# A decoder step on one core: where the values are stored from, who clears the padded attention tiles, and the pauses of the index list

## The chip, the cores and the metric

One core of a Trainium2 chip runs the whole program. The metric is device time in microseconds per execution; lower is better. Engines are named as in the profile: PE (TensorE, matmuls), DVE (VectorE), ACT (ScalarE), POOL (GpSimd), SP (SyncE, which here only issues DMAs).

## What is computed

Two layers over 256 prompt tokens and 8 x 4 sample tokens that share all weights (width 2048, float32). Layer 0 is sparse attention, layer 1 a Conformer convolution; each is followed by a ConvFFN and layer norms. The change lies in layer 0, and of it this matters:

```python
def one_seq(q_s, qi_s, wi_s, ki_s, k_new, v_new, pages):
    idx, valid = index_select(qi_s, wi_s, ki_s, pos_new, key_pos, k_sel)   # top 256 of 2052 keys, per token
    ...
    k_s = jnp.where(in_past, cache_k[phys, off], k_new[new_idx])
    v_s = jnp.where(in_past, cache_v[phys, off], v_new[new_idx])
    return attend_selected(q_s, k_s, v_s, valid)
```

For each of the 32 sample tokens an indexer scores 2052 keys and the best 256 are attended to; their keys and values lie in a paged cache and are gathered by row. The prompt tokens attend under a mask made from their own top 64. The new keys and values k, v are outputs as well.

## The kernel before

**Weights.** Every projection is a list of groups, each cut into slabs of 512 KB that SP loads into five buffers (`raw`). A float32 product is made of three passes over split operands: ACT makes the high part `wh` of a slab (L162), DVE or, for slabs marked `pool`, POOL makes the low part `wl` (L164), and PE multiplies (L231 to L233). `pump` issues loads five slabs ahead and splits up to three ahead, with three buffers for `wh` and `wl`.

**Order.** The order of the instructions on every engine is the order of the Python code; nothing is reordered later. While PE's matmuls are written, `tick` counts their nominal time as credit and runs generators in several lanes. A generator's `yield 2.5` means: go on after 2.5 us of credit. So the pauses set where the small work stands between the matmuls, on all engines, but each engine waits only for its data.

**The list of selected keys.** `sample_index` scores the keys, finds the 256th largest score by bisection (31 rounds on DVE with a small PE product each), and then, behind this threshold, makes the list: ranks among equals (L926), the selection (L929 to L933), a prefix sum (L939) with its count (L941), the sum of the counts on PE (L878, L948), nine compaction steps (L953 to L956), eight shift steps (L980, L981), a product on PE that puts the list together (L987) and the index tile `idxS` (L990). All this runs while PE multiplies the last slabs of q and of v.

**Gathers.** `kv_load` issues row gathers on POOL, two per token, each followed by a small memset as a pause, into a ring of 9 tokens: 4 buffers of `kvA` (two tokens until the projections end), 3 of `kvB`, and 2 in `kvx`, which takes over the memory of `xl`. A slot is refilled when its token's values have been used. `idxS` lets the first gather go.

**Values.** The projection's result is copied by ACT to `vT` (in the memory of `qi`), stored from there by SP, transposed by PE, and copied to `vt` and `vs`, which last through the attention. Then the pools of the indexer are closed, and the attention's tiles (`cp`) take over their memory.

**Attention.** A loop over the 32 tokens transposes the gathered keys (`keys`, L1207, copied out to `KT` by ACT at L1212 and DVE at L1210), makes scores of the token before (L1220 to L1228) with queries in the padded tile `qz` (L1313), and after four tokens a softmax and the values with padded weights in `PTz` (L1271). The padded tiles are cleared once (L1138), and later only their diagonals are written. Between these steps a filler does the prompt's attention: masked score products (L1156, L1157), maxima on DVE (L1158), exponentials on ACT (L1162), transposes (L1183, copied to `PT` by ACT), value products (L1179). The filler runs alone until `HEAD` us of its work are written, then the token loop starts.

Of the kernel before, what the change touches and what calls it, by code (L numbers as in the profile page):

```python
# [7 lines left out]
F32 = mybir.dt.float32  # L8
# [8 lines left out]
D = 2048  # L17
NT = 16
TP = 256
NS, TS = 8, 4  # L20
T = TP + NS * TS
NH, HD, NKV, GQ = 16, 128, 4, 4
NI, ID = 16, 64
# [3 lines left out]
FF = 5632  # L27
NF = FF // 128
CW = 31
# [8 lines left out]
NKVB = 3  # L38
# [8 lines left out]
KXD = (53.0, 4.8)  # L47
PRW = (6.0, 14.0, 9.0)
DOT = 0.35
HEAD = 3.0  # L50
DOTW = 5.0
PEM, NACT = 3, 4
BIS = (1.4, 0.3)
# [483 lines left out]
def trunk(ctx, tc, a, o, stages=9):  # L537
    k = K(ctx, tc, a, o)
    nc = k.nc
    base = k.base  # L540
# [6 lines left out]
    g_q = [k.add(Group([(win, QC + 512 * i, 512)], [128] * 4, NT, 2)) for i in range(4)]  # L547
    g_v = [k.add(Group([(win, VC + 256 * i, 256)], [128] * 2, NT, 4)) for i in range(2)]
    for g in g_q[1:]:
        for s_ in g.slabs[:8 if g is not g_q[3] else 4]:  # L550
            s_.pool = True
    def halving(w, nk):
        return [k.add(Group([(w, 512 * i, 512)], [128] * 4, nk, 2)) for i in range(3)] + \
# [40 lines left out]
    def hilo():  # L594
        xh = base.tile([128, NT, T + 2], F32R, name="xh")
        xl = base.tile([128, NT, T + 2], F32R, name="xl")
        return xh, xl

    xh, xl = hilo()
# [39 lines left out]
    def cc(n, p0=0, p1=128):  # L639
        o_, w_ = CO[n] if n in CO else CI[n]  # L640
        return (con if n in CO else coni)[p0:p1, o_:o_ + w_]
# [15 lines left out]
    def gather(out, src, idx):  # L657
        nc.gpsimd.indirect_dma_start(out=out, out_offset=None, in_=src,  # L658
                                     in_offset=bass.IndirectOffsetOnAxis(ap=idx, axis=0))
# [90 lines left out]
    kvt = {"pos": 0, "done": 0, "cap": 2}  # L750
    RING = 4 + NKVB + 2

    def kv_load(done):
        kvt["done"] += done
        while kvt["pos"] < min(kvt["done"] + kvt["cap"], NS * TS):
            t = kvt["pos"]
            i = t % RING - 4 - NKVB
            if i < 0:
                g = (kvA if i + NKVB < 0 else kvt["B"]).tile([128, 2, 1024], F32, name="kvt")
            else:  # L760
                g = kvt["B2"][:, i]
            kvt[t] = g
            for c in range(2):
                gather(g[:, c], a["kvc"], idxS[:, 32 * c + t:32 * c + t + 1])

                nc.gpsimd.memset(pause, 0)
            kvt["pos"] += 1
# [57 lines left out]
    def sample_index():  # L825
# [3 lines left out]
        p = pb()  # L829
# [13 lines left out]
        for pr in range(4):  # L843
# [3 lines left out]
            for i in range(4):  # L847
                p = pb()
# [8 lines left out]
        p = pb()  # L857
# [8 lines left out]
        p = pb()  # L866
# [7 lines left out]
        v = sp.tile([128, 1], I32, name="v", bufs=2)  # L874

        def total():
            p_ = pb()
            nc.tensor.matmul(p_[:, :1], cc("bones"), cnt, start=True, stop=True)  # L878
            return p_
# [3 lines left out]
        p = total()  # L883
# [9 lines left out]
        for bit in range(30, -1, -1):  # L893
# [8 lines left out]
            p = total()  # L902
# [5 lines left out]
        v = cand  # L908
# [8 lines left out]
        p = total()  # L917
# [6 lines left out]
        nc.vector.tensor_scalar(need, need, float(KSEL_S), None, op0=OP.add)  # L924
        rank = sp.tile([128, W1], I16, name="scr", bufs=2)
        nc.vector.tensor_tensor_scan(rank, eq, eq, 0.0, OP.add, OP.max)  # L926
        yield 2.5

        nc.vector.scalar_tensor_tensor(eq, rank, need[:, 0:1], eq, op0=OP.is_le, op1=OP.mult)  # L929
        nc.vector.tensor_tensor(gt, gt, eq, op=OP.add)  # L930
# [2 lines left out]
        nc.vector.tensor_tensor(mbS[96:128, KSEL_S:].rearrange("p (b t) -> p b t", t=TS),  # L933
                                new[96:128, None, :].to_broadcast([32, NS, TS]),
                                cc("blk", 96, 128).rearrange("p (b t) -> p b t", t=TS), op=OP.max)
        yield 2.0

        r = sp.tile([128, 512], I16, name="scr", bufs=2)
        nc.vector.tensor_tensor_scan(r, gt[:, :512], zer, -1.0, OP.add, OP.add)  # L939
# [3 lines left out]
        nc.vector.scalar_tensor_tensor(f, r, -32768.0, code, op0=OP.mult, op1=OP.add)  # L943
        x_ = sp.tile([128, 512], I32, name="x_", tag="w", bufs=3)
        nc.vector.tensor_tensor(x_, f, gt[:, :512], op=OP.mult)
        yield 1.5
        p = total()
        nc.tensor.matmul(p[:, 1:2], cc("lower"), cnt, start=True, stop=True)  # L948

        for b in range(9):  # L950
            s_ = 1 << b
            m = sp.tile([128, 512], I32, name="m_", tag="w", bufs=3)
            nc.vector.tensor_scalar(m, x_, 1 << (15 + b), None, op0=OP.bitwise_and)  # L953
            y = sp.tile([128, 512], I32, name="x_", tag="w", bufs=3)
            nc.vector.scalar_tensor_tensor(y, m, 0.0, x_, op0=OP.is_equal, op1=OP.mult)
            nc.vector.copy_predicated(y[:, :512 - s_], m[:, s_:], x_[:, s_:])  # L956
            x_ = y
            yield 2.6

        tot = sp.tile([128, 2], F32, name="tot")  # L960
        nc.vector.tensor_copy(tot, p[:, :2])
# [15 lines left out]
        for b in range(8):  # L977
            s_ = 1 << b
            y = sp.tile([128, KSEL_S], F32, name="lst", tag="w", bufs=3)
            nc.vector.tensor_scalar(y, lst, b0[:, b:b + 1], None, op0=OP.mult)  # L980
            nc.vector.scalar_tensor_tensor(y[:, s_:], lst[:, :KSEL_S - s_], b1[:, b:b + 1], y[:, s_:],  # L981
                                           op0=OP.mult, op1=OP.add)
            lst = y
            yield 1.2
        p = pb()
        for c in range(2):
            nc.tensor.matmul(p[:, 32 * c:32 * c + 32], lst[:, 128 * c:128 * c + 128], cc("bones")[:, :32],  # L987
                             start=True, stop=True)
        yield 0.7
        nc.vector.tensor_scalar(idxS, p[:, :64], 0.25, None, op0=OP.add)  # L990
        kv_load(0)

# [65 lines left out]
    vt = ap.tile([128, 2, 512], F32, name="vt")  # L1058
    vs = ap.tile([32, 512], F32, name="vs")
# [5 lines left out]
    for gi in range(2):  # L1065
# [4 lines left out]
        pl_.append(prompt_index(gi))  # L1070

    k.bg.append(sample_index())


# [9 lines left out]
    vT = bp.tile([128, 8, T], F32, name="qi")  # L1084

    def turn_v(gi):

        for tt in range(3):
            n = 128 if tt < 2 else 32
            p = pb()  # L1090
            for m in range(2):
                nc.tensor.transpose(p[:n, m * 128:m * 128 + 128], vT[:, 2 * gi + m, tt * 128:tt * 128 + n], ident)
            dst = vt[:, tt] if tt < 2 else vs
            nc.scalar.activation(dst[:, 256 * gi:256 * gi + 256], p[:n, :256], AF.Copy)
            yield 0.6

    for gi in range(2):
        ps = k.gemm(g_v[gi], xin, pg)
        for m in range(2):
            nc.scalar.activation(vT[:, 2 * gi + m], ps[m][:, :T], AF.Copy)  # L1100
        nc.sync.dma_start(o["v"].rearrange("(j p) t -> p j t", p=128)[:, 2 * gi:2 * gi + 2], vT[:, 2 * gi:2 * gi + 2])
        if gi:
            k.drain(k.ev, k.bg2, kxl, pl_, k.bg)
        pl_.append(turn_v(gi))
    k.drain(pl_)
    k.lanes.remove(kxl)
    k.lanes.remove(pl_)
    k.fine = False
# [7 lines left out]
    kvB = stC.enter_context(tc.tile_pool(name="kvB", bufs=NKVB))  # L1116
# [2 lines left out]
    def bank(n, bufs):  # L1119
        return pp.tile([128, 512], F32, name=n, bufs=bufs)  # L1120

    kvt["B"] = kvB
    kvt["cap"] = 4 + NKVB
    kv_load(0)


    ot = q
    kvt["B2"], kvt["cap"] = base.tile([128, 2, 2, 1024], F32, name="kvx", tag="xl"), RING
    kv_load(0)
    qz = [cp.tile([128, TS, NKV, 16], F32, name=f"qz{i}", bufs=1) for i in range(2)]  # L1130
    PTz = [cp.tile([128, 2, TS, NKV, 16], F32, name=f"PTz{i}", bufs=1) for i in range(2)]

# [2 lines left out]
        return bass.AP(tensor=t.tensor, offset=t.offset + off, ap=[list(t.ap[0]), [68, TS], [16, NKV], [1, GQ]])  # L1135

    for t in qz + PTz:
        nc.gpsimd.memset(t, 0.0)  # L1138

    def filler():  # L1140
        units = [(tt, h) for tt in range(2) for h in range(4)]
# [152 lines left out]

    while owed[0] < HEAD:
        r = next(fl)
# [548 lines left out]
    return a  # L1845


_OUT = {"y": (D, T), "k": (512, T), "v": (512, T), "kidx": (ID, T), "conv_p": (128, NT * (CW - 1)), "conv": (128, NT * NS * (CW - 1 + TS)), "ffn": (2, FF, 18)}


def build(a):
    import concourse.bacc as bacc
    nc = bacc.Bacc("TRN2", target_bir_lowering=False, num_devices=1)
    ins = {n: nc.dram_tensor(n, v.shape, mybir.dt.from_np(v.dtype), kind="ExternalInput").ap() for n, v in a.items()}
    outs = {n: nc.dram_tensor("out_" + n, s, F32, kind="ExternalOutput").ap() for n, s in _OUT.items()}
    with tile.TileContext(nc) as tc:
        with ExitStack() as ctx:
            trunk(ctx, tc, ins, outs)
    return nc


def _unlayout(r):
    c = np.ascontiguousarray
    t = lambda v: (v[:, :TP].T, v[:, TP:].T)
    yp, ys = t(r["y"])
    kp, ks = t(r["k"])
    vp, vs = t(r["v"])
    ip, is_ = t(r["kidx"])
    ff = r["ffn"]
    cp = r["conv_p"].reshape(128, NT, CW - 1).transpose(2, 1, 0)  # L1870
    cs = r["conv"].reshape(128, NT, NS, CW - 1 + TS)[..., TS:].transpose(2, 3, 1, 0)
    return (c(yp).reshape(1, TP, D), c(ys).reshape(NS, TS, D),
            c(kp).reshape(1, 1, TP, NKV, HD), c(vp).reshape(1, 1, TP, NKV, HD), c(ip).reshape(1, 1, TP, ID),
            c(cp).reshape(1, 1, CW - 1, D), c(ff[:, :, :2].transpose(0, 2, 1)).reshape(2, 1, 2, FF),
            c(ks).reshape(1, NS, TS, NKV, HD), c(vs).reshape(1, NS, TS, NKV, HD), c(is_).reshape(1, NS, TS, ID),
            c(cs).reshape(1, NS, CW - 1, D), c(ff[:, :, 2:].transpose(0, 2, 1)).reshape(2, NS, 2, FF))
# [8 lines left out]
```

## Time and profile before

| | us |
|---|---|
| median of 3 runs | 2647.25 (2644.3 to 2649.05) |
| the profiled execution, its own time | 2651.09 |
| its span, first to last instruction | 2649.3 |
| PE busy in the span | 2554.9 (96%) |
| DVE busy | 1623.9 (61%) |
| ACT busy | 1164.5 (44%) |
| POOL busy | 647.4 (24%) |

The times in the rows below are counted from the start of the span. A timeline row has the start, the length, the engine, the line and the operation with its output and inputs; in brackets stands how long the engine had stood before it, and what released it. The granted clock (PEclk) is 1.00 at 2.4 GHz and 0.50 at 1.2 GHz.

### The profile page before, as it was taken

The numbers are of one execution on the slowest core, as the hardware profiler recorded it, in microseconds if no ns is written. First come the engines' busy times: TensorE is split into PE (matmuls) and PEld (weight loads), VectorE is DVE, ScalarE is ACT, GpSimd is POOL, SyncE is SP. The second block draws the span as 40 slices with busy tenths as digits, with TensorE's granted clock in tenths as the row PEclk, the third lists the DMA queues.
The fourth block names the chain that finished last, engine by engine and source line by source line (L and its number), as shares of the span: only waits on it lengthen the run. The fifth ranks groups of instructions, "written<-read, shape, count | busy, mean of one in ns | idle before, by whom it ended". The sixth has DMA issues, their size and how long they took to land.

```text
span 2649.3 us, 49606 instructions
## 1 busy us (share of the span) xinstructions
PE 2554.9 (96%) x19608; PEld 2454.3 (93%) x19608; DVE 1623.9 (61%) x2536; ACT 1164.5 (44%) x1811; POOL 647.4 (24%) x921
## 2 busy tenths in 40 slices
PE   8999789999999999999998999899999999999997
PEld 8888556999999999999998889899999999999997
DVE  4577444777665445555558888779555444555554
ACT  4434334455444334344346444656444333444334
POOL 2033362342222101111036444344101000101123
PEclk9999899999999999999999999999999999999999
DMA  9834576456554455554645677455555445555643
GB/s 342 196 104 128 215 238 224 159 163 200 171 161 167 164 168 160 168 166 153 180 160 141 161 188 194 149 168 155 169 168 162 165 162 168 162 171 160 173 160 107
DMA packets 410553, 454.91 MB, mean 172 GB/s; under 512 B 34816, under 2 KB 338608, under 8 KB 409168
## 3 DMA queue, kind: packets, MB, share of 16 engines
q1 hardware_dynamic: 397920, 400.66, 49.4%
q0 software_dynamic: 12400, 51.09, 5.7%
q8 instruction: 153, 2.51, 0.4%
q14 instruction: 80, 0.66, 0.1%
HBM read 438.37 MB, written 13.30 MB: 170 GB/s over the span
## 4 chain that ended last, share of the span: by engine, by line
PE 89%; DVE 4%; POOL 2%; DMA 2%; ACT 1%; issue 1%; SPq 0%; ACTq 0%; DVEq 0%; POOLq 0%
PE pt L233 25%; PE pt L232 25%; PE pt L231 25%; PE pg L231 2%; PE pg L233 2%; PE pg L232 2%; PE pt L1671 1%; PE tr L1207 1%; DVE wl L164 1%; ACT wh L162 1%; PE m L1271 1%; POOL kvt L658 1%; DMA xt<-spread 1%; PE pg L849 1%; PE sc L1228 1%
## 5 line engine op out<-in xcount | busy, mean ns | idle before, releaser
L164 DVE TENSOR_TENSOR wl<-raw,wh 128x1024 fp32r<-128x1024 f32 (+2 forms) x705 | 879.3, 1250 | 781.0 <-ACT wh L162 768.3
L162 ACT ACTIVATE wh<-raw 128x1024 fp32r<-128x1024 f32 (+1 forms) x726 | 760.5, 1051 | 917.8 <-PE pt L232 682.1
L233 PE MATMUL pt<-xh,wl 128*128 128x288 f32 (+1 forms) x3520 | 1040.8, 296 | 4.1 <-DVE wl L164 4.1
L231 PE MATMUL pt<-xh,wh 128*128 128x288 f32 (+1 forms) x3520 | 1043.0, 296 | 0.8 <-ACT xh L1330 0.8
L232 PE MATMUL pt<-xl,wh 128*128 128x288 f32 (+1 forms) x3520 | 1043.1, 296 | 0.1
L233 PEld LDWEIGHTS pt<-xh,wl 128*128 128x128 f32 x3520 | 666.9, 189 | 5.1 <-DVE wl L164 5.1
L231 PEld LDWEIGHTS pt<-xh,wh 128*128 128x128 f32 x3520 | 664.1, 189 | 7.4 <-issue 5.8
L232 PEld LDWEIGHTS pt<-xl,wh 128*128 128x128 f32 x3520 | 664.6, 189 | 0.5 <-DVE xl L1331 0.3
L233 PE MATMUL pt<-hh,wl 128*128 128x288 f32 (+1 forms) x1664 | 495.4, 298 | 2.9 <-DVE wl L164 2.9
L231 PE MATMUL pt<-hh,wh 128*128 128x288 f32 (+1 forms) x1664 | 493.2, 296 | 1.2 <-ACT wh L162 1.2
L232 PE MATMUL pt<-hl,wh 128*128 128x288 f32 (+1 forms) x1664 | 493.2, 296 | 0.0
L1446 POOL COPY sto<-gpad 128x2 f32<-128x2 f32 x88 | 82.0, 932 | 962.1 <-ACT gpad L1439 962.0
L233 PEld LDWEIGHTS pt<-hh,wl 128*128 128x128 f32 x1664 | 312.7, 188 | 3.9 <-DVE wl L164 3.9
L231 PEld LDWEIGHTS pt<-hh,wh 128*128 128x128 f32 x1664 | 313.5, 188 | 2.4 <-ACT wh L162 2.1
L232 PEld LDWEIGHTS pt<-hl,wh 128*128 128x128 f32 x1664 | 313.9, 189 | 0.2
L231 PE MATMUL pg<-xh,wh 128*128 128x288 f32 (+1 forms) x528 | 167.1, 317 | 8.6 <-ACT wh L162 8.6
L233 PE MATMUL pg<-xh,wl 128*128 128x288 f32 (+1 forms) x528 | 158.0, 299 | 1.7 <-DVE wl L164 1.7
L232 PE MATMUL pg<-xl,wh 128*128 128x288 f32 (+1 forms) x528 | 158.0, 299 | 0.1
L1450 ACT ACTIVATE s<-y,pvec 128x304 f32<-128x304 f32 x88 | 48.5, 551 | 161.6 <-DVE y L1445 161.6
L231 PEld LDWEIGHTS pg<-xh,wh 128*128 128x128 f32 (+1 forms) x528 | 100.5, 190 | 17.9 <-ACT wh L162 8.8
L233 PEld LDWEIGHTS pg<-xh,wl 128*128 128x128 f32 (+1 forms) x528 | 100.4, 190 | 3.1 <-DVE wl L164 3.1
L232 PEld LDWEIGHTS pg<-xl,wh 128*128 128x128 f32 (+1 forms) x528 | 100.4, 190 | 2.9 <-issue 2.4
(377 smaller groups left out, 2323.2 us busy)
## 6 DMA issues: line engine op xcount, KB each, us to landing
raw<-w_ffn_gate SPq DMA_DIRECT2D x352, 256.0 KB, 2.9
raw<-w_ffn_up SPq DMA_DIRECT2D x352, 256.0 KB, 3.2
raw<-w_ffn_down SPq DMA_DIRECT2D x169, 512.0 KB, 3.5
raw<-w_attn_in SPq DMA_DIRECT2D x64, 512.0 KB, 5.7
raw<-w_pw SPq DMA_DIRECT2D x128, 256.0 KB, 4.5
raw<-w_attn_out SPq DMA_DIRECT2D x32, 512.0 KB, 5.3
raw<-w_pw SPq DMA_DIRECT2D x32, 512.0 KB, 3.6
xt<-spread SPq DMA_DIRECT2D x60, 136.0 KB, 2.9
```

The lines of the kernel that those rows point to most:

```text
L162: nc.scalar.activation(wh[:, :n], r[:, :n], AF.Copy)
L164: eng.tensor_tensor(wl[:, :n], r[:, :n], wh[:, :n].bitcast(F32), op=OP.subtract)
L231: nc.tensor.matmul(out, wh[:, c:c + w], xh, start=st, stop=False)
L232: nc.tensor.matmul(out, wh[:, c:c + w], xl, start=False, stop=False)
L233: nc.tensor.matmul(out, wl[:, c:c + w], xh, start=False, stop=sp)
L658: nc.gpsimd.indirect_dma_start(out=out, out_offset=None, in_=src, in_offset=bass.IndirectOffsetOnAxis(ap=idx, axis=0))
L849: nc.tensor.matmul(p[:, :512], qb[:, pr], kx[pr][:, 512 * i:512 * i + 512], start=True, stop=True)
L1207: nc.tensor.transpose(p[:, h * 128:(h + 1) * 128], g[:, h * 128:(h + 1) * 128], ident)
L1228: nc.tensor.matmul(p[32 * h:32 * h + 16, :KSEL_S], qz[b % 2][:, i, h], kt[:, h], start=False, stop=(i == TS - 1), skip_group_check=True)
L1271: nc.tensor.matmul(po[32 * h:32 * h + 16, :128], z[:, c, i, h], g[:, 512 + h * 128:640 + h * 128], start=False, stop=(i == TS - 1 and c == ...
L1446: nc.gpsimd.tensor_copy(sto[:, j, 0:2], gp[:, 256:258])
L1450: nc.scalar.activation(s[:, :304], y[:, :304], AF.Silu, bias=k.par(bc, j))
```

## The change

Six edits, all in the attention layer:

- the values are stored once, at the end of the projections, from `vt` and `vs`, in rows by token instead of by column (the host no longer transposes them); the store from `vT` is gone;
- `qz` and `PTz` are cleared by DVE instead of POOL, and in front of the gathers that follow the projections instead of behind them; the two calls of `kv_load` there become one;
- of the slabs of q's last group two instead of four are split by POOL, the other two by DVE;
- the first three pauses behind the threshold are 1.0 us longer each;
- the nine pauses of the compaction are 0.4 us shorter, the eight of the shifts 0.2 us, and the one in front of `idxS` is gone;
- `HEAD` is 2.0 instead of 3.0.

```diff
-HEAD = 3.0
+HEAD = 2.0
...
     for g in g_q[1:]:
-        for s_ in g.slabs[:8 if g is not g_q[3] else 4]:
+        for s_ in g.slabs[:8 if g is not g_q[3] else 2]:
             s_.pool = True
...
         nc.vector.tensor_tensor_scan(rank, eq, eq, 0.0, OP.add, OP.max)
-        yield 2.5
+        yield 3.5
...
-        yield 2.0
+        yield 3.0
 
         r = sp.tile([128, 512], I16, name="scr", bufs=2)
...
         nc.vector.tensor_tensor(x_, f, gt[:, :512], op=OP.mult)
-        yield 1.5
+        yield 2.5
         p = total()
...
             nc.vector.copy_predicated(y[:, :512 - s_], m[:, s_:], x_[:, s_:])
             x_ = y
-            yield 2.6
+            yield 2.2
...
             lst = y
-            yield 1.2
+            yield 1.0
         p = pb()
         for c in range(2):
             nc.tensor.matmul(p[:, 32 * c:32 * c + 32], lst[:, 128 * c:128 * c + 128], cc("bones")[:, :32],
                              start=True, stop=True)
-        yield 0.7
         nc.vector.tensor_scalar(idxS, p[:, :64], 0.25, None, op0=OP.add)
         kv_load(0)
...
             nc.scalar.activation(vT[:, 2 * gi + m], ps[m][:, :T], AF.Copy)
-        nc.sync.dma_start(o["v"].rearrange("(j p) t -> p j t", p=128)[:, 2 * gi:2 * gi + 2], vT[:, 2 * gi:2 * gi + 2])
         if gi:
             k.drain(k.ev, k.bg2, kxl, pl_, k.bg)
         pl_.append(turn_v(gi))
     k.drain(pl_)
+
+    nc.sync.dma_start(o["v"][:TP].rearrange("(a p) c -> p a c", p=128), vt)
+    nc.sync.dma_start(o["v"][TP:], vs)
...
+    for t in qz + PTz:
+        nc.vector.memset(t, 0.0)
+
+
     kvt["B"] = kvB
-    kvt["cap"] = 4 + NKVB
-    kv_load(0)
-
-
-    ot = q
     kvt["B2"], kvt["cap"] = base.tile([128, 2, 2, 1024], F32, name="kvx", tag="xl"), RING
     kv_load(0)
...
-    for t in qz + PTz:
-        nc.gpsimd.memset(t, 0.0)
...
-    vp, vs = t(r["v"])
+    vp, vs = r["v"][:TP], r["v"][TP:]
```

How it moves instructions shows at three places. The first is the start of the list on DVE, from the ranks to the count (`rsh` is the rope of q, `wl` a weight split). Before:

```order
L926 SCALAR_TENSOR_TENSOR scr<-eq 128x516
L722 STREAM_SHUFFLE rsh<-rsh 128x288
L723 TENSOR_TENSOR rsh<-rsh,con 128x288
L724 TENSOR_TENSOR rsh<-rsh,con 128x288
L726 TENSOR_TENSOR rsh<-rsh 128x288
L929 SCALAR_TENSOR_TENSOR eq<-scr,need,eq 128x516
L930 TENSOR_TENSOR gt<-gt,eq 128x516
L932 TENSOR_SCALAR new<-gt 32x4
L933 TENSOR_TENSOR mbS<-new,con 32x32
L939 SCALAR_TENSOR_TENSOR scr<-gt,zer 128x512
L941 TENSOR_SCALAR cnt<-scr 128x1
```

Now, the same piece:

```order
L926 SCALAR_TENSOR_TENSOR scr<-eq 128x516
L164 TENSOR_TENSOR wl<-raw,wh 128x1024
L722 STREAM_SHUFFLE rsh<-rsh 128x288
L723 TENSOR_TENSOR rsh<-rsh,con 128x288
L724 TENSOR_TENSOR rsh<-rsh,con 128x288
L726 TENSOR_TENSOR rsh<-rsh 128x288
L929 SCALAR_TENSOR_TENSOR eq<-scr,need,eq 128x516
L930 TENSOR_TENSOR gt<-gt,eq 128x516
L932 TENSOR_SCALAR new<-gt 32x4
L933 TENSOR_TENSOR mbS<-new,con 32x32
L164 TENSOR_TENSOR wl<-raw,wh 128x1024
L939 SCALAR_TENSOR_TENSOR scr<-gt,zer 128x512
```

The two splits that POOL made stand in DVE's order now, one ahead of the rope and one ahead of the scan; on PE the sum of the counts (L878) moves back by 24 matmuls, and L987 forward by 24.

The second place is DVE from the index to the filler's first maxima. Before:

```order
L990 TENSOR_SCALAR idxS<-pg 128x64
L1158 TENSOR_REDUCE mx<-tr 128x4
L1160 TENSOR_SCALAR mx<-mx 128x4
L1166 RECIPROCAL sm<-sm 128x4
L1168 TENSOR_SCALAR P<-P,sm 128x128 x4
```

Now:

```order
L989 TENSOR_SCALAR idxS<-pg 128x64
L164 TENSOR_TENSOR wl<-raw,wh 128x1024 x2
L1133 MEMSET qz_3176 128x256
L1133 MEMSET qz_3177 128x256
L1133 MEMSET PTz_3178 128x512
L1133 MEMSET PTz_3179 128x512
L1158 TENSOR_REDUCE mx<-tr 128x4
```

One split that stood ahead of the index stands behind it, and the four memsets, on POOL behind eighteen gathers before, stand on DVE ahead of the first maximum.

The third place is PE behind the projections, after the first eight score products of the filler. The difference:

```order
 L1157 MATMUL tr<-kT,x 128x128
-L1183 MATMUL tr<-ident,P 128x128 x4
-L1179 MATMUL q<-PT,vt 128x512
 L1207 MATMUL tr<-ident,kvt 128x128 x4
-L1156 LDWEIGHTS identN
-L1156 MATMUL tr<-pm,identN 128x128
-L1157 MATMUL tr<-kT,x 128x128
```

The first transposes of gathered keys (L1207) stand ahead of the transposes of the first softmax (L1183), where they stood behind its value product.

## Rows read from the trace of the kernel before

**Rows 1.** The page's chain that ended last, shares by engine.

```profile
PE 89%; DVE 4%; POOL 2%; DMA 2%; ACT 1%; issue 1%; SPq 0%; ACTq 0%; DVEq 0%; POOLq 0%
```

**Rows 2.** Windows of 5 us: length, PE, PEld, DVE, ACT, POOL busy (instructions), PEclk, DMA, GB/s.

```profile
235.00:240.00 5.00, 3.38 (x14) 3.41 (x15) 4.56 (x8) 0.00 (x0) 0.00 (x0) 0.50 0.41 120
...
295.00:300.00 5.00, 1.80 (x5) 1.14 (x6) 2.86 (x12) 2.36 (x12) 4.34 (x9) 0.61 1.04 416
...
305.00:310.00 5.00, 0.00 (x0) 0.00 (x0) 0.00 (x0) 0.00 (x0) 4.34 (x9) 0.97 1.02 419
...
315.00:320.00 5.00, 4.93 (x27) 2.29 (x27) 1.75 (x7) 2.62 (x9) 0.00 (x0) 0.50 0.40 163
```

**Rows 3.** Timeline, PE in the list: start, length, line, operation, [idle before <-releaser].

```profile
236.62 0.56 PE L878 MATMUL pg<-cnt,con 128*128 128x1 f32 x2 [5.17 <-DVE cnt L941]
...
282.94 0.70 PE L987 MATMUL pg<-con,lst 128*128 128x32 f32 x4
...
287.02 0.30 PE L233 MATMUL pg<-xh,wl 128*128 128x288 f32 x1
```

**Rows 4.** Timeline, DVE from the last split before the index.

```profile
285.12 1.22 DVE L164 TENSOR_TENSOR wl<-raw,wh 128x1024 fp32r<-128x1024 f32 x1 [1.94 <-ACT wh L162]
...
286.26 0.22 DVE L990 TENSOR_SCALAR idxS<-pg 128x64 int32<-128x64 f32 x1
...
292.80 0.69 DVE L1158 TENSOR_REDUCE mx<-tr 128x4 f32<-128x512 f32 x1 [6.32 <-DMA out_v<-qi]
...
312.99 1.20 DVE L1313 COPY qz<-qn 128x64 f32<-128x64 f32 x1 [12.94 <-POOL qz L1138]
```

**Rows 5.** Timeline, POOL: gathers and memsets.

```profile
286.76 1.07 POOL L658 DMA_INDIRECT kvt<-kvc,idxS  x1 [51.98 <-DVE idxS L990]
...
311.43 0.95 POOL L658 DMA_INDIRECT kvx<-kvc,idxS  x1 [0.17 <-issue]
...
312.62 0.58 POOL L1138 MEMSET qz<- 128x256 f32 x2
...
335.37 0.95 POOL L658 DMA_INDIRECT kvt<-kvc,idxS  x1 [21.23 <-PE m L1271]
```

**Rows 6.** Timeline, PE at the start of the attention.

```profile
289.13 0.22 PE L1156 MATMUL tr<-pm,identN 128*128 128x128 bf16 x1 [0.56 <-ACT vs L1094]
...
291.51 0.44 PE L1157 MATMUL tr<-kT,x 128*128 128x128 f32 x2
...
299.47 2.08 PE L1179 MATMUL q<-PT,vt 128*128 128x512 f32 x2 [2.25 <-ACT PT L1185]
...
315.07 1.11 PE L1183 MATMUL tr<-ident,P 128*128 128x128 f32 x4 [10.15 <-DVE KT L1210]
...
319.08 0.42 PE L1220 MATMUL sc<-mbS,selB 32*128 32x288 bf16 x1
...
343.60 1.09 PE L1207 MATMUL tr<-ident,kvt 128*128 128x128 f32 x8
```

**Rows 7.** Timeline, POOL's last weight split.

```profile
232.44 2.34 POOL L164 TENSOR_TENSOR wl<-raw,wh 128x1024 fp32r<-128x1024 f32 x1 [0.19 <-ACT wh L162]
```

**Rows 8.** Timeline, DVE at the start of the list.

```profile
227.51 0.48 DVE L722 STREAM_SHUFFLE rsh<-rsh 128x288 f32<-128x288 f32 x1
...
232.57 2.23 DVE L932 TENSOR_SCALAR new<-gt 32x4 bf16<-32x4 int16 x1
...
235.06 1.22 DVE L939 TENSOR_TENSOR_SCAN scr<-gt,zer 128x512 int16<-128x512 int16 x1
```

**Rows 9.** Timeline, ACT in the list and at token 0's keys.

```profile
228.29 1.08 ACT L162 ACTIVATE wh<-raw 128x1024 fp32r<-128x1024 f32 x1
...
229.44 1.84 ACT L729 ACTIVATE x<-rsh 32x288 f32<-32x288 f32 x4
...
302.44 0.60 ACT L1212 ACTIVATE KT<-tr 128x512 f32<-128x512 f32 x1 [0.26 <-issue]
```

**Rows 10.** Waits of DVE, 235 to 284 us: total, times, longest.

```profile
DVE wl L164 <- ACT wh L162: 3.8, 5, 1.9
```

More of the change, by code (lines that the diff above doesn't have):

```diff
@@ L1120, in bank @@
         return pp.tile([128, 512], F32, name=n, bufs=bufs)
-    kvt["B"] = kvB
-    kvt["cap"] = 4 + NKVB
-    kv_load(0)
     ot = q
-    kvt["B2"], kvt["cap"] = base.tile([128, 2, 2, 1024], F32, name="kvx", tag="xl"), RING
-    kv_load(0)
     qz = [cp.tile([128, TS, NKV, 16], F32, name=f"qz{i}", bufs=1) for i in range(2)]
@@ L1137, in trunk @@
     for t in qz + PTz:
-        nc.gpsimd.memset(t, 0.0)
+        nc.vector.memset(t, 0.0)
+    kvt["B"] = kvB
+    kvt["B2"], kvt["cap"] = base.tile([128, 2, 2, 1024], F32, name="kvx", tag="xl"), RING
+    kv_load(0)
     def filler():
@@ L1845, in _layout @@
     return a
-_OUT = {"y": (D, T), "k": (512, T), "v": (512, T), "kidx": (ID, T), "conv_p": (128, NT * (CW - 1)), "conv": (128, NT * NS * (CW - 1 + TS)), "ffn": (2, FF, 18)}
+_OUT = {"y": (D, T), "k": (512, T), "v": (T, 512), "kidx": (ID, T), "conv_p": (128, NT * (CW - 1)), "conv": (128, NT * NS * (CW - 1 + TS)), "ffn": (2, FF, 18)}
 def build(a):
```

## The prediction

> **What bounds the kernel now.** The page's chain of waits gives PE 89% of the span [rows 1], so an edit to the attention layer can only give time where PE stands. I looked for such places in the 5 us stretches, then followed each on the other engines.
>
> Two places show. In 235 to 240 us PE is busy 3.38 of 5.00 us at a granted clock of 0.50. Between 295 and 320 it does 1.80 of 5.00, then nothing in 305 to 310, and comes back at a clock of 0.50 [rows 2].
>
> At the first place PE waits 5.17 us for the count that the list's prefix sum makes on DVE [rows 3]. At the second, DVE stands 6.32 us at L1158 until the store out_v<-qi has landed, and 12.94 us at L1313 until POOL has cleared qz [rows 4]. POOL clears the tiles only after eighteen gathers, issued from 286.76 to 311.43 [rows 5]. Behind L1313 in DVE's order stand the copies that free PSUM, so PE waits 10.15 us at 315.07 [rows 6]. Transfers are no bound there: POOL has issued all it may and stands 21.23 us before the next gather [rows 5].
>
> **Part one, the list (222 to 287 us).** Two weight splits go from POOL to DVE, the first pauses get longer, the later ones shorter.
>
> The later of the two took 2.34 us on POOL [rows 7]; while it ran, DVE's L932, on 32x4 elements, took 2.23 us [rows 8], and L930 before it was long in the same way. Both get shorter, but this gives nothing, since the second moved split stands between them and the scan L939 and must wait for ACT. In order: ACT's wh runs from 228.29, 1.08, to 229.4 [rows 9]. The first split, 1.14 from start to start (L164 at 285.12 to the next at 286.26 [rows 4]), ends at 230.6. The rope, 1.93 from its first operation to ACT's L729 [rows 8, 9], brings 232.5; L729 x4, 1.84, 234.4; ACT's next wh 235.4; the second split 236.6. So L939 starts at 236.6 instead of 235.06 [rows 8], and the count, which let PE go 1.56 later at 236.62 [rows 3], is there at 238.1. The longer pauses put PE's sum of the counts 24 matmuls further back, 0.13 us each (27 between L987's end and 287.02 [rows 3]): PE comes there at 231.45 + 3.2 = 234.7 and stands 3.4 us instead of 5.17. That is 1.8 us, and up to 1.7 of clock (half of the 3.38 at 0.50).
>
> It does not last, since DVE sets the rest. From L939 to the end of PE's L987, which takes the finished list, passed 235.06 to 283.64, 48.6 us [rows 3, 8]; in 3.8 of them DVE waited for wh [rows 10]. With the pauses shortened one split fewer stands in between (1.1), and PE is ahead of DVE, so no wait for wh: 48.6 - 3.8 - 1.1 = 43.7. L987 ends at 280.3, 3.3 us earlier. But it stands 24 rows earlier in the value product, so PE waits there some 3 us, and 51 matmuls follow, 6.7 us: the last projection matmul ends at 287.1, against 287.3 now. **Term one: -0.2 us**; the 24 rows give back what the list gained. With no wait of PE at L987 it would be -3.5, with DVE's 3.8 of waits still there +3.6. I take the middle, because the list's rows leave DVE no gap.
>
> What the list does give is the index, no longer behind a split that waits for ACT: written at about 280.6 instead of 286.48, first gather at 280.9 instead of 286.76.
>
> **Part two, the attention's start (287 to 320 us).** The v store no longer reads qi, whose memory the attention's tiles take over, so DVE's first maximum waits only for PE: eight score products run from 289.13 to 291.95 [rows 6], four are through after 1.4 us, and with term one DVE starts at 288.9 + 1.4 = 290.3 instead of 292.80: 2.5 us.
>
> The four memsets stand on DVE just ahead. DVE has none in the trace. Below, they cost nothing beside that wait; above, four times the 0.69 of a 128x512 operation [rows 4] are 2.8. POOL's two qz took 0.58 [rows 5], the PTz have twice the elements: 1.7 in all, which I take, being the same tiles. They may start once PE has read qi for the last time, at 288.9 at the latest, and end by 290.6; so between nothing and 0.3 shows (1.4 at 2.8), and I take nothing. The Trainium skill (VectorE: DVE Perf Modes, section "Zero memsets can be issued as uint32 (trn2)") gives one cycle per element; 1536 elements at the skill's 0.96 GHz would be 1.6 us, an estimate from the page that no row here shows on DVE.
>
> From the first maximum to the end of the first value product passed 292.80 to 301.55, 8.75 us [rows 4, 6]; ACT now copies one KT tile, 0.60 [rows 9], ahead of PT, so it ends at 290.3 + 9.35 = 299.65. Then come eight key transposes (1.1, as at 343.60 [rows 6]) and four score products (1.4), and L1313 waits for nobody. Token 0's scores (L1220) begin at 302.15 instead of 319.08, 16.9 us earlier, term one among them. With HEAD at 2, one unit's transposes and value product are not done by then and follow later; their rows at the low clock are 1.11 and 2.08 [rows 6], half of that 1.6, with gaps 1.8. **Term two: -16.9 + 1.8 + 0.2 = -14.9 us.**
>
> The gathers keep up. The first of the second burst was issued at 335.37, and PE transposed it at 343.60 [rows 5, 6]: at most 8.2 us to land. So the first lands by 289.1, and PE wants it at 291.7. The eighteenth, 17 times 1.45 later, lands by 313.8; PE comes to token 9's keys 24.5 us behind token 0's scores [rows 6], to token 8's about 21, at 323. The v stores still carry 576 KB, now all of it beside the gathers; 288 KB more at 419 GB/s [rows 2] are 0.7 us, under that cover. Behind token 8 every refill waits for a token that PE has used, so the pattern moves as one. On SP the loads that no longer stand behind the store come earlier and nobody awaits them. All behind the layer is the same work.
>
> **Sum.** -0.2 - 14.9 = -15.1 us. The profiled execution took 2651.09 us (span 2649.3), 3.8 above the median of 2647.25; it would take 2636.0, and the median **2632**.
>
> **The rivals.**
>
> *More (0.14).* PE does not wait at L987, as DVE takes the list faster than its old rows say: 3.3 us more, and the clock of 0.61 in 295 to 300 stays at 1.00, some 2 us: 2627. Against it: the sum leaves DVE no gap.
>
> *Keys ahead of the first softmax (0.08).* PE takes its order as it stands, and token 0's key transposes now come before the first softmax's. If the first gather, with 288 KB of stores and weights beside it, lands 14 us after its issue instead of 8.2, that is at 294.9, PE stands 3.2 us; if the index is no earlier than before, 9 us: 2635 to 2641. Against it: the 8.2.
>
> *Nothing (0.05).* The wait only changes its name. The memsets wait for four of POOL's DMA queues. I read these as the index gathers of the start, since the first maximum waited for the same four and was released by the store. Were they the new gathers, DVE would stand until those land: gain 0 to 2, about 2646.
>
> *Slower (0.03): the clock.* PE's work after 289 comes in pieces with gaps. The granted clock was 0.61 in 295 to 300, where PE worked 1.80 of 5.00 us, and 0.50 in 315 to 320, after it had stood for ten, though it was then busy 4.93 of 5.00 [rows 2]. If it stays at the lower level, 1.2 GHz, from the first score product through token 8, the 21 us of work from token 0's scores take 42, and the 13 before some 3 more: -15.1 + 24 = +8.9, so 2656. It decides from the point where the gaps between tokens are as long as those around 295. Against it: once the keys are in, PE's next piece is always ready. The Trainium skill (TensorE: Matmul & The Clock Gate, Part 1) says "the default state is throttled, and activity releases the throttle"; by that rule a scattered start could hold the clock down, and the trace agrees as far as the 0.50 goes.
>
> **The numbers.** The forecast has 0.70. Its own range, from term one (-3.5 to +3.6), the memsets (1.4), the clock (2) and the runs' spread (2.4 either way), is 2626 to 2638. For 8 in 10 I take 2625 to 2641, which takes in the first two rivals but for a tail. A measurement can tell about 0.2%, 5.3 us: faster is under 2642, slower over 2652.5. Faster 0.70 + 0.14 + 0.07 = 0.91, same 0.06, slower 0.03.
>
> **What would show it.** Right: no wait of DVE on out_v or POOL between 285 and 320; PE's wait at L878 near 3.4 us, one at L987 near 3; first gather near 280.9; last projection matmul near 287; token 0's scores near 302; all behind token 8 some 15 us earlier. Wrong: a long wait of PE on a gather at the first key transposes, or of DVE at the memsets; the last projection matmul over 4 us off; or the 15 us given back behind token 8, where refills and not PE would set the pace.

## The result, and the profile after

| kernel | median of runs, us | range | profiled execution | its span |
|---|---|---|---|---|
| before | 2646.40 (6 runs) | 2643.76 to 2649.05 | 2651.09 | 2649.3 |
| after | 2632.98 (6 runs) | 2630.60 to 2634.12 | 2634.12 | 2632.3 |

The ratio is 0.9941, 95% interval 0.9931 to 0.9951: 13.4 us by the medians. The two profiled executions are 17.0 us apart, because that of before lies above all six of its runs; in which stage is shown below.

The changed kernel's 5 us stretches, in the columns of [rows 2]:

```profile
235.00:240.00 5.00, 1.62 (x10) 1.38 (x9) 3.58 (x5) 2.55 (x4) 0.00 (x0) 0.89 0.24 64
240.00:245.00 5.00, 5.00 (x21) 5.00 (x22) 4.18 (x6) 1.06 (x1) 0.00 (x0) 0.50 0.48 149
...
295.00:300.00 5.00, 1.94 (x9) 1.30 (x10) 3.30 (x13) 2.48 (x10) 4.50 (x7) 0.69 1.02 386
300.00:305.00 5.00, 5.00 (x22) 3.64 (x22) 1.40 (x3) 1.19 (x2) 4.34 (x9) 0.62 1.04 416
305.00:310.00 5.00, 4.09 (x47) 2.71 (x47) 3.05 (x8) 2.86 (x11) 3.71 (x6) 1.00 1.03 415
```

The stretch from 305 to 310, in which PE did nothing before, is 4.09 us busy now. What is left is in 295 to 305: two softmax steps in a row, and a granted clock of 0.69 and 0.62. DVE's timeline answers to [rows 4]:

```profile
281.86 0.22 DVE L989 TENSOR_SCALAR idxS<-pg 128x64 int32<-128x64 f32 x1 [0.50 <-PE pg L987]
...
290.15 0.55 DVE L1133 MEMSET qz<- 128x256 f32 x2 [2.42 <-PE pg L1091]
290.75 1.03 DVE L1133 MEMSET PTz<- 128x512 f32 x2
292.11 0.69 DVE L1158 TENSOR_REDUCE mx<-tr 128x4 f32<-128x512 f32 x1 [0.33 <-issue]
...
296.95 0.28 DVE L1313 COPY qz<-qn 128x64 f32<-128x64 f32 x1
```

Neither the wait for out_v nor the one for POOL is there. The clearings take 1.58 us and are over by 291.78, about when PE's first four score products are. PE's timeline, with POOL's behind it, answers to [rows 3, 5, 6]:

```profile
238.95 0.59 PE L878 MATMUL pg<-cnt,con 128*128 128x1 f32 x2 [3.38 <-DVE cnt L941]
...
281.12 0.70 PE L987 MATMUL pg<-con,lst 128*128 128x32 f32 x4 [1.19 <-DVE lst L980]
...
290.53 0.22 PE L1156 MATMUL tr<-pm,identN 128*128 128x128 bf16 x1 [0.56 <-ACT vs L1093]
...
293.19 0.60 PE L1207 MATMUL tr<-ident,kvt 128*128 128x128 f32 x4
...
295.88 0.79 PE L1183 MATMUL tr<-ident,P 128*128 128x128 f32 x4 [2.10 <-ACT P L1162]
...
298.85 1.11 PE L1207 MATMUL tr<-ident,kvt 128*128 128x128 f32 x4 [2.18 <-ACT P L1162]
...
299.82 2.08 PE L1179 MATMUL q<-PT,vt 128*128 128x512 f32 x2
...
305.00 0.29 PE L1220 MATMUL sc<-mbS,selB 32*128 32x288 bf16 x1
```

```profile
282.37 1.06 POOL L658 DMA_INDIRECT kvt<-kvc,idxS  x1 [54.96 <-DVE idxS L989]
...
307.73 0.94 POOL L658 DMA_INDIRECT kvx<-kvc,idxS  x1 [0.17 <-issue]
...
322.50 0.94 POOL L658 DMA_INDIRECT kvt<-kvc,idxS  x1 [13.45 <-PE m L1271]
```

Token 0's scores (L1220) start at 305.00, against 319.08 [rows 6]. PE finds its first keys ready at 293.19 (L1207, no wait in brackets); what it waits for now is ACT's exponentials, 2.10 and 2.18 us.

**Where the 17 us lie.** The two executions are already 0.93 us apart at L922, DVE's first operation behind the bisection, which the change leaves alone (224.98, 225.91). So every profile is counted from its own L922. The columns are starts, in us behind it: the first gather, the first score product (L1156), token 0's scores (L1220), the first value product of a request (L1271), the output projection (L231 on pt), and the end of the span. The "row stretch" is the time from L1271 to the output projection.

| profile | gather | score pr. | token 0 | L1271 | projection | end | row stretch |
|---|---|---|---|---|---|---|---|
| before | 61.8 | 64.2 | 94.1 | 109.5 | 214.2 | 2424.3 | 104.7 |
| after | 56.5 | 64.6 | 79.1 | 95.7 | 193.0 | 2406.4 | 97.3 |
| e13, before again | 61.9 | 64.2 | 94.1 | 109.6 | 204.4 | 2417.5 | 94.9 |
| e10, after again | 54.9 | 63.1 | 77.5 | 94.1 | 192.1 | 2404.9 | 98.0 |

The second profile of before agrees with the first to 0.1 us up to L1271, and is then 9.9 us shorter in the row stretch. So the apparent gain of 7.4 us there (104.7 to 97.3) does not belong to the change. After and e10 differ as well: by 1.6 us at token 0's scores, which goes back to the list and the clock in it (see "Why the prediction was right").

### The profile page after: what moved, and what is told of

It is laid out like the page before. It is cut to its first block, busy times and chain, and to the rows that moved or that the text cites. A ratio compares the mean times of both kernels' runs of the same rounds, so it can differ in the third digit from the quotient of the medians.

```text
span 2632.3 us, 49607 instructions
## 1 busy us (share of the span) xinstructions
PE 2553.5 (97%) x19608; PEld 2456.2 (93%) x19608; DVE 1624.8 (62%) x2542; ACT 1163.3 (44%) x1811; POOL 640.4 (24%) x915
## 4 chain that ended last, share of the span: by engine, by line
PE 87%; DVE 4%; DMA 3%; POOL 3%; ACT 2%; issue 1%; SPq 0%; ACTq 0%; DVEq 0%; POOLq 0%
PE pt L233 25%; PE pt L232 25%; PE pt L231 25%; PE pg L231 2%; PE pg L233 2%; PE pg L232 2%; DVE wl L164 1%; DMA kvt<-kvc,idxS 1%; PE pt L1671 1%; PE tr L1207 1%; ACT wh L162 1%; PE pg L849 1%; POOL x L489 1%; PE pg L1009 0%; PE m L1271 0%
## 5 line engine op out<-in xcount | busy, mean ns | idle before, releaser
L164 DVE TENSOR_TENSOR wl<-raw,wh 128x1024 fp32r<-128x1024 f32 (+1 forms) x707 | 882.0, 1251 | 783.0 <-ACT wh L162 770.9
L231 PE MATMUL pt<-xh,wh 128*128 128x288 f32 (+1 forms) x3520 | 1042.6, 296 | 0.8 <-ACT xh L1330 0.8
L231 PEld LDWEIGHTS pt<-xh,wh 128*128 128x128 f32 x3520 | 663.5, 189 | 7.8 <-issue 5.4
L231 PE MATMUL pt<-hh,wh 128*128 128x288 f32 (+1 forms) x1664 | 493.2, 296 | 1.2 <-ACT wh L162 1.2
L231 PEld LDWEIGHTS pt<-hh,wh 128*128 128x128 f32 x1664 | 313.6, 188 | 2.4 <-ACT wh L162 2.1
L231 PE MATMUL pg<-xh,wh 128*128 128x288 f32 (+1 forms) x528 | 168.3, 319 | 7.7 <-ACT wh L162 7.7
L231 PEld LDWEIGHTS pg<-xh,wh 128*128 128x128 f32 (+1 forms) x528 | 101.6, 192 | 16.9 <-issue 8.4
```

The source lines that it names most:

```text
L164: eng.tensor_tensor(wl[:, :n], r[:, :n], wh[:, :n].bitcast(F32), op=OP.subtract)
L231: nc.tensor.matmul(out, wh[:, c:c + w], xh, start=st, stop=False)
```

## The experiments

They ran in three batches, on three chips, on which the kernel before took 2656.5 us (e1 to e4), 2658.0 (e5, e6, e7, e9) and 2647.4 (e10 to e13); the ratios are against the kernel before on the same chip. The last three columns come from one profiled execution each, counted from L922 as above.

| run | what is different | median, us | ratio (95%) | token 0 | projection | row stretch |
|---|---|---|---|---|---|---|
| e1 | before, DVE clears | 2650.44 | 0.9978 (0.9969 to 0.9987) | 87.6 | 208.6 | 105.8 |
| e2 | before, store from vt, vs | 2655.77 | 0.9996 (0.9987 to 1.0005) | 94.2 | 214.5 | 104.8 |
| e3 | before, both | 2648.37 | 0.9972 (0.9961 to 0.9983) | 83.5 | 206.5 | 105.4 |
| e4 | before, list alone | 2651.27 | 0.9977 (0.9968 to 0.9986) | 90.6 | 213.6 | 107.3 |
| e5 | after, HEAD 3 | 2641.05 | 0.9943 (0.9929 to 0.9957) | 82.8 | 200.4 | 102.7 |
| e6 | after, POOL clears | 2640.52 | 0.9937 (0.9923 to 0.9950) | 77.2 | 203.0 | 106.3 |
| e7 | after, count later | 2642.17 | 0.9947 (0.9933 to 0.9961) | 79.0 | 204.0 | 107.3 |
| e9 | before, HEAD 2 | 2653.90 | 0.9991 (0.9982 to 1.0000) | 80.7 | 212.9 | 104.7 |
| e10 | after | 2633.25 | 0.9944 (0.9930 to 0.9958) | 77.5 | 192.1 | 98.0 |
| e11 | after, no pause | 2629.89 | 0.9931 (0.9919 to 0.9943) | 79.3 | 190.3 | 94.7 |
| e12 | after, old list | 2633.56 | 0.9945 (0.9933 to 0.9957) | 80.1 | 193.3 | 96.7 |
| e13 | before | 2648.01 | 1.0004 (0.9995 to 1.0012) | 94.1 | 204.4 | 94.9 |

**e1, VectorE clears.**

```diff
-        nc.gpsimd.memset(t, 0.0)
+        nc.vector.memset(t, 0.0)
```

> The kernel before, with one word changed: VectorE instead of GpSimd clears qz and PTz; store, list and HEAD as before. Theory A (the clearing behind the eighteen gathers is the bound, the store a smaller one ahead of it): DVE's wait for POOL at L1313 (12.94 us) is gone, the wait for out_v near 6.3 us stays and moves to the first clearing, the clearing itself (1.6 us) now shows: -12.9 + 1.6 = -11.3, so about 2635 against 2646. Theory B (clearing only hides a later wait, on the gathers or on PE's own order): under 3 us, 2643 to 2646.

6 us, half of what theory A expected. DVE's timeline in e1:

```profile
295.84 0.55 DVE L1138 MEMSET qz<- 128x256 f32 x2 [6.41 <-PE tr L1157]
296.44 1.02 DVE L1138 MEMSET PTz<- 128x512 f32 x2
297.38 0.63 DVE L1158 TENSOR_REDUCE mx<-tr 128x4 f32<-128x512 f32 x1
...
304.65 0.60 DVE L1313 COPY qz<-qn 128x64 f32<-128x64 f32 x1
```

POOL's wait is gone, as expected, and the store's wait has moved ahead of the clearing. The bracket names PE, but SP's timeline speaks for the store, in before and then in e1:

```profile
287.79 0.38 SPq L1101 DMA_DIRECT2D out_v<-qi  x1
```

```profile
290.75 0.38 SPq L1101 DMA_DIRECT2D out_v<-qi  x1
```

In before it was issued 5.0 us ahead of the maximum that it held (292.80), in e1 5.1 us ahead of the clearing (295.84). The size is not as expected: the 12.94 us were DVE's. PE, which sets the end, was still busy until about 305 in before and stood 10.15 [rows 6]. Take away the first maximum's delay of 2.3 us (70.1 against 67.8 behind L922) and some 8 are left; token 0's scores came 6.6 us earlier than in e2 beside it.

**e2, the store alone.**

```diff
-        nc.sync.dma_start(o["v"].rearrange("(j p) t -> p j t", p=128)[:, 2 * gi:2 * gi + 2], vT[:, 2 * gi:2 * gi + 2])
...
+    nc.sync.dma_start(o["v"][:TP].rearrange("(a p) c -> p a c", p=128), vt)
+    nc.sync.dma_start(o["v"][TP:], vs)
```

> The kernel before, with the value store from vt and vs alone; POOL still clears. Theory A: DVE's wait for out_v at L1158 (6.32 us) is gone and the first maximum comes near 290, but DVE then stands that much longer at L1313 for POOL, which still clears near 312.6: 0, within 1 us of 2646. Theory B (the store is what holds the start): -6, so 2640.

As theory A said: DVE's first maximum no longer waits for the store, and DVE's wait for POOL grows:

```profile
312.20 1.20 DVE L1315 COPY qz<-qn 128x64 f32<-128x64 f32 x1 [13.48 <-POOL qz L1140]
```

By itself the store gives 0.7 us, and the interval reaches past 1.

**e3, store and clearing:** the lines of e1 and of e2 together.

> The kernel before with both: store from vt and vs, VectorE clears; pauses, weight splits and HEAD as before. Theory A (the two waits add once both are gone, and list, splits and HEAD are worth next to nothing): -13 to -15, 2631 to 2633, the same as the whole change. Theory C (the part of the gain that shows only behind token 8, some 7 us in the profiles, comes from HEAD = 2, the order of prompt work and tokens): PE's small gaps behind token 8 stay, -8 to -10, 2636 to 2638.

The time, -8.1 us, is in the range of theory C; e5 and e9 test that theory directly.

**e4, the list alone:** in the kernel before, the pauses and the splits of the change.

```diff
-        for s_ in g.slabs[:8 if g is not g_q[3] else 4]:
+        for s_ in g.slabs[:8 if g is not g_q[3] else 2]:
...
-        yield 2.5
+        yield 3.5
...
-            yield 2.6
+            yield 2.2
```

> The kernel before, with the other pauses and the two weight splits on VectorE alone; store, clearing and HEAD as before. Theory A: PE waits 3.4 us instead of 5.2 at L878 and some 1.2 us at L987, the first gather is issued about 5 us earlier, POOL clears 5 us earlier (near 307.7 instead of 312.6), so DVE's wait at L1313 falls from 12.9 to about 8: -4 to -5, near 2641.5, by way of POOL and not of the list. Theory D (the list's own time counts): PE's last projection matmul 1 us later than in the kernel before and nothing else: 2646 to 2648.

-5.2 us, near what theory A said (-4 to -5), and by way of POOL. Timelines of POOL and of DVE in e4:

```profile
311.12 0.57 POOL L1137 MEMSET qz<- 128x256 f32 x2
```

```profile
311.48 1.20 DVE L1312 COPY qz<-qn 128x64 f32<-128x64 f32 x1 [7.73 <-POOL qz L1137]
```

DVE waits 7.73 us instead of 12.94. The earlier index lets POOL through its gathers earlier: it clears 84.2 us behind L922 instead of 87.6, 3.4 earlier (theory A said 5). The rest of the shorter wait is DVE's own: its first maximum came 1.6 us later. Token 0's scores come 3.5 us earlier (90.6 against 94.1); where the other 1.7 us of the time lie, this profile does not show. In the changed kernel nobody waits for POOL there, so this gain cannot be had a second time.

**e5 and e9, HEAD.** e5 is the changed kernel with the first line of this, e9 the kernel before with the second.

```diff
-HEAD = 2.0
+HEAD = 3.0
...
-HEAD = 3.0
+HEAD = 2.0
```

> The changed kernel with HEAD back at 3. Theory C (the gain behind token 8 comes from HEAD = 2; in the four runs with HEAD = 3 the stretch from the first value product of a request to the layer's output projection takes 104.7 to 107.3 us, in the changed kernel 97.3): that stretch goes back to about 105, and token 0's scores come 2 to 4 us later: 6 to 11 us slower than the changed kernel, so 2% is never in question but the ratio to the kernel before is 0.9965 to 0.9985 instead of 0.994. Theory A (store, clearing and list make the gain): within 1.5 us of the changed kernel.

> The kernel before with HEAD = 2 alone. Theory C: DVE still stands at L1313 until POOL has cleared (near 312.6), token 0's scores hardly move, and the stretch from the first value product of a request to the output projection falls from 105 to about 97 us: 5 to 8 us faster than the kernel before. Theory A: within 1.5 us of it.

Theory C falls: the changed kernel keeps its ratio with HEAD = 3 (0.9943; 2641.05 us, beside 2640.52 and 2642.17 in e6 and e7 with HEAD = 2), and HEAD = 2 alone gives 0.9 in a thousand, at the edge of the interval, with a row stretch of 104.7. In e9 token 0's L1220 runs early, at 80.7, but the scores behind it then wait for the keys, whose copy stands behind DVE's wait for POOL:

```profile
315.12 1.06 PE L1228 MATMUL sc<-KT,qz 128*16 128x256 f32 x8 [9.82 <-DVE KT L1210]
```

So the first value product (L1271) comes at 108.3, against 109.5. The profiles of e5 and e6, which also differ in who clears, show what HEAD does in the changed kernel: with HEAD = 2 token 0's scores are 5.6 us earlier (77.2 against 82.8), and by the output projection all of it has been given back (203.0 against 200.4). The edit of HEAD gives the whole nothing that these runs can tell.

**e6, POOL clears at the new place.**

```diff
-        nc.vector.memset(t, 0.0)
+        nc.gpsimd.memset(t, 0.0)
```

> The changed kernel with GpSimd clearing again, at the new place ahead of the second load of rows (so behind eight gathers and not eighteen). If the place is what counts: POOL clears near 294 to 296, DVE waits for nothing at L1313, DVE's 1.6 us of clearing ahead of the first maximum are gone, ten gathers go out 1.7 us later: within 1.5 us of the changed kernel. If the engine is what counts: DVE waits for POOL again, 3 us slower or more.

The place counts, not the engine: 0.9937 (0.9923 to 0.9950) against 0.9944 (0.9930 to 0.9958) for the changed kernel itself (e10, on another chip). POOL's timeline in e6:

```profile
288.14 0.56 POOL L1133 MEMSET qz<- 128x256 f32 x2 [1.21 <-ACT vt L1093]
288.64 1.00 POOL L1133 MEMSET PTz<- 128x512 f32 x2
...
289.80 0.94 POOL L658 DMA_INDIRECT kvt<-kvc,idxS  x1 [0.15 <-issue]
```

It clears behind four gathers (the expectation said eight) and in the same time as DVE, 1.56 us.

**e7, the count later.**

```diff
-        p = total()
-        nc.tensor.matmul(p[:, 1:2], cc("lower"), cnt, start=True, stop=True)
         for b in range(9):
...
-            yield 2.2
+            yield 2.4
+        p = total()
+        nc.tensor.matmul(p[:, 1:2], cc("lower"), cnt, start=True, stop=True)
         tot = sp.tile([128, 2], F32, name="tot")
```

> The changed kernel, with PE's sum of the counts (L878) issued behind the nine steps of the list that do not need it, and those steps' pause at 2.4 instead of 2.2. Theory E (PE's 3.4 us at L878 and the low clock behind it are lost for nothing): no wait at L878, some 2 to 4 us at L987, the first score product 2 to 4 us earlier, and the same at the end. Rival F (the attention's start then waits for the first gather, which lands 4 us or more behind its issue, or for the exponentials of ACT): the first score product earlier, token 0's scores not, 0 to 1 us in all.

Neither theory holds: the first score product itself is not earlier (64.4 behind L922, against 63.1 in e6 beside it). Waits of PE in e7, 225 to 292 us (total, times, longest), then its stretches:

```profile
PE pg L987 <- DVE lst L980: 2.5, 1, 2.5
PE pg L233 <- DVE wl L164: 1.5, 3, 0.9
```

```profile
240.00:245.00 5.00, 4.65 (x35) 4.42 (x34) 4.90 (x8) 1.45 (x2) 0.00 (x0) 1.00 0.50 156
...
280.00:285.00 5.00, 4.48 (x19) 4.49 (x20) 1.26 (x5) 1.06 (x1) 2.69 (x4) 0.52 0.19 44
```

The 3.4 us at L878 are gone and the clock stays up behind it, but PE now waits for the weight splits and longer for the list, and the low clock (0.52) comes behind that wait. The list's end is no earlier for it (L987 ends 55.6 us behind L922, in e6 54.4): where PE stands in this stretch has changed, and not when the list is done.

**e10 and e13, both kernels again,** without an edit.

> The changed kernel itself, on the chip of the experiments. Theory K (the 97.3 us from the first value product of a request to the output projection, against 103 to 107 in eight other profiles, belong to one execution or one chip): here that stretch is 103 to 107, and the ratio still 0.994. Theory L (it belongs to the kernel): near 97, and the ratio below 0.992.

> The kernel before itself, on the chip of the experiments, for its stages: the ratio is 1 within 0.1%; token 0's scores near 94 us behind L922 and the stretch from the first value product of a request to the output projection near 105, as on the first chip.

The ratio is 0.9944, as on the first chip. Neither theory of e10 was whole: the row stretch is 98.0, as in the first profile of after, but 94.9 in before, so it is neither an accident of that one execution nor a merit of the change. It goes with PE's gaps that the profile puts down to "issue", that is, to no wait that it can name: in the profile of before and in e1 to e9 they come to 2.7 to 8.2 us between 300 and 440, with a row stretch of 102.7 to 107.3; in after and e10 to e13 there are none, and it is 94.7 to 98.0. PE's waits in before's row stretch (334.43 to 439.16 us):

```profile
PE m L1271 <- issue: 2.3, 8, 0.3
PE tr L1207 <- issue: 2.0, 2, 1.1
```

These gaps are not all of it: the same 512 value products (L1271) are 22.99 us busy in before's row stretch and 19.41 in that of e13. And the medians of the kernel before differ between the batches by about as much as its row stretch does between the two profiles: 2656.5 and 2658.0 against 2647.4, and 9.9 us. What holds PE there, and why only in some batches, stays open.

**e11, no pause between gathers.**

```diff
-                nc.gpsimd.memset(pause, 0)
```

> The changed kernel without POOL's pause (a clearing of 0.33 us) between two gathers, so that they go out every 1.1 us instead of 1.44. Theory G (the supply of gathered rows sets the pace behind token 0): the last of the first eighteen leaves 5 to 6 us earlier, the stretch to the output projection is 3 to 8 us shorter, and so is the end. Rival H (PE's own chain through ACT and DVE sets it): within 1.5 us of the changed kernel, or slower, where more transfers at once slow each other.

3.4 us below e10 in medians, with intervals that overlap (0.9919 to 0.9943, 0.9930 to 0.9958), and a row stretch 3.3 shorter. The eighteenth gather left no earlier, though: 80.4 us behind L922, against 80.3, since POOL stood before the last two until earlier ones had landed:

```profile
302.66 0.94 POOL L658 DMA_INDIRECT kvx<-kvc,idxS  x1 [0.75 <-DMA kvt<-kvc,idxS]
305.74 0.94 POOL L658 DMA_INDIRECT kvx<-kvc,idxS  x1 [2.14 <-DMA kvt<-kvc,idxS]
```

In the row stretch PE waits 2.0 us for gathered rows, in e10 4.9, which is most of the 3.3. So the supply matters a little behind token 8 in these two profiles; that e11 beats the changed kernel is likely and not shown. It is faster than the kernel before.

**e12, the old list in the changed kernel:** e4's lines the other way round.

> The changed kernel with the pauses and the two weight splits of before. By the prediction's term one (-0.2 us) it is the same as the changed kernel. By the difference of the two runs with HEAD = 3 (0.9972 with the old list, 0.9943 with the new one) it is 6 to 8 us slower, its first gather 6 us later, and PE waits for that gather at token 0's key transposes, ahead of the first softmax.

0.3 us slower than e10: term one of the prediction stands. The first gather is 7.5 us later (62.4 against 54.9), and yet PE does not wait for it (no bracket at L1208). Timelines of POOL and PE in e12:

```profile
290.09 1.06 POOL L658 DMA_INDIRECT kvt<-kvc,idxS  x1 [52.58 <-DVE idxS L990]
```

```profile
295.12 0.60 PE L1208 MATMUL tr<-ident,kvt 128*128 128x128 f32 x4
```

Within 5.0 us of its issue the gather has landed. This leaves e3 unexplained: store, clearing and old list with HEAD = 3 gave 8.1 us, the same with HEAD = 2 (e12) 13.8, while HEAD alone gives little in e5. e3's token 0 is where e5's is (83.5, 82.8), and the rest is lost behind it (projection 206.5, 200.4). The late index does not show there as a wait: in the row stretch PE waits 1.6 us for gathered rows in e3 and 2.2 in e5. Part of the loss is the same products taking longer (those into `sc` between token 0's first scores and the first value product are 5.84 us busy, in e5 4.25). Whether that is HEAD together with a late index, or the other chip, was not separated.

## Why the prediction was right

The forecast was the likeliest case, 2632.0 us (2625 to 2641); measured were 2632.98, and -13.4 (here) and -14.1 us (e10's batch, 2647.39 to 2633.25) against the predicted -15.1. The mechanism came out as forecast, and one term was mis-sized. The steps, by e13 and e10, which have no "issue" gaps:

- **Term one (-0.2).** The whole list part is worth 0.3 us (e12). PE's wait at L878 is 3.38, as forecast (3.4). The one at L987 is 1.2 and not 3. I had let PE gain up to 1.7 us of clock behind L878 and DVE run without waiting for wh; in after neither held. The low clock came behind L878 all the same (in 240 to 245 the granted clock was 0.50 in after and 0.66 in e10), and the list moves with it: in after DVE waits twice more for ACT's wh (0.75 and 0.38 us; in e10 not at all), and both PE and the list come to L987 1.5 us later. It ends 55.9 (after) and 54.4 us (e10) behind L922, forecast 55.3. The index, forecast 55.6 behind L922, came at 55.9 and 54.4.
- **DVE's two waits** are gone. The first maximum, forecast 65.3 behind L922, came at 66.2 and 64.7.
- **The clearings**, taken at 1.7 us and hidden, take 1.58 and are hidden: with POOL doing them (e6), token 0's scores are 0.3 us earlier than in e10. The estimate from the Trainium skill (VectorE: DVE Perf Modes, section "Zero memsets can be issued as uint32 (trn2)") was 1.6, and the trace agrees.
- **Token 0's scores**, forecast 16.9 us earlier, are 16.6 earlier in e10 (94.1 to 77.5) and 15.0 in after (79.1).
- **Given back:** the one term that was mis-sized. Forecast were 1.8 us for the unit of prompt work that HEAD = 2 defers; measured are 1.1 by L1271 (16.6 to 15.5) and 3.2 more in the row stretch (94.9 to 98.0): 4.3. Counted in the same way it is 3.6 in after and 2.8 in e12, so the size is sure to 1 or 2 us only. That it belongs to HEAD is what e5 against e6 suggests. Part is work that HEAD moved there: PE is busy 89.55 us of that stretch in e10, 87.61 in e13. Part is the supply, which I had said keeps up: PE's waits there for gathered rows, in e13 and then in e10, total, times and longest:

```profile
PE tr L1207 <- DMA kvt<-kvc,idxS: 2.8, 5, 1.3
PE tr L1207 <- DMA kvx<-kvc,idxS: 1.3, 1, 1.3
```

```profile
PE tr L1207 <- DMA kvt<-kvc,idxS: 3.7, 6, 1.1
PE tr L1207 <- DMA kvx<-kvc,idxS: 1.2, 1, 1.2
```

  0.8 us more. "The pattern moves as one" was thus 2 to 3 us too good (the row stretch is 96.7, 97.3 and 98.0 in e12, after and e10, against 94.9), and the sign named for it (the gain given back behind token 8) is there on a small scale. At the projection 12.3 us of e10's gain are left; the medians say 14.1, and e13's profiled execution (2645.28) was 2.7 us faster than the median of its kernel.

Of the rivals, *Keys ahead of the first softmax* is out: PE transposes the first keys at 293.19 without a wait, and even with the late index (e12). *Nothing* is out, as the clearings wait for PE alone. *Slower* is out: the granted clock is 0.69 and 0.62 in 295 to 305, and 1.00 in the 5 us behind. *More* needed no wait at L987; there is one.

What the parts give alone does not show in the sum. Store 0.7, clearing 6.0 and list 5.2 us add up to 12 by themselves, but the list shortened the same wait for POOL that the clearing takes away, and in the whole change it is worth 0.3.

## What to carry to other kernels

Price a removed wait by what the engine that sets the end stands there, not by what the waiting engine stands: DVE's 12.94 us were 10.15 of PE's, and taking it away gave 6.0 of the total (e1). Clear buffers ahead of a long queue of issues on the same engine; which engine cleared them then made no difference here (e6). Before a gain in a later stage is booked, take a second profile of the same unchanged kernel: here it moved by 9.9 us in one stage between two executions.

## What the runs showed of the hardware

Two of the first gathers took longer on POOL while DVE split weights. POOL's and DVE's timelines in e10:

```profile
282.74 1.44 POOL L658 DMA_INDIRECT kvt<-kvc,idxS  x1 [0.17 <-issue]
...
284.67 0.95 POOL L658 DMA_INDIRECT kvt<-kvc,idxS  x1 [0.17 <-issue]
...
286.11 1.25 POOL L658 DMA_INDIRECT kvt<-kvc,idxS  x1 [0.17 <-issue]
```

```profile
282.11 1.23 DVE L164 TENSOR_TENSOR wl<-raw,wh 128x1024 fp32r<-128x1024 f32 x1 [1.22 <-ACT wh L162]
285.31 1.22 DVE L164 TENSOR_TENSOR wl<-raw,wh 128x1024 fp32r<-128x1024 f32 x1 [1.98 <-ACT wh L162]
```

The gathers took 1.44 and 1.25 us where 0.95 is usual. Each had started while a DVE operation of 1.23 us with two inputs, both in SBUF, ran, and each ended 0.83 to 0.84 us after that operation did. In e11 the overlap is longer, and so is the gather; it too ends 0.84 us after DVE:

```profile
281.60 1.23 DVE L164 TENSOR_TENSOR wl<-raw,wh 128x1024 fp32r<-128x1024 f32 x1 [1.34 <-ACT wh L162]
...
281.91 1.76 POOL L658 DMA_INDIRECT kvt<-kvc,idxS  x1 [0.30 <-issue]
```

So these gathers were held until the operation was over. The one at 284.67, under way when DVE's began at 285.31, took its usual 0.95. The Trainium skill (SBUF — State Buffer, section "Who interferes with whom") says that a VectorE instruction with two SBUF inputs contends with a GpSimd instruction that reads SBUF; the trace agrees, a gather reading its indices there. The same section of the Trainium skill infers that `tensor_tensor` does not hold up the making of a DMA's descriptors on GpSimd; the gather as a whole was held here, and which part of it no run separates. And a clearing of 128x256 or 128x512 takes the same time on POOL as on DVE (0.56 and 1.00 us for two on POOL in e6, 0.55 and 1.03 on DVE in after).
